# Expert products in split parts for whole tiles of one expert, with a shorter ring of weights

## Chip, cores and metric

The kernel runs on one core of one Trainium2 chip. The metric is the device time of one execution in microseconds (us).

## The reference, cut to what matters

Two trunk layers run over 256 latent tokens and 256 context tokens of 1024 features in float32. Each has a token-mixing part and a channel-mixing part. The channel mixing of the second layer, on the latent tokens alone, is a top-2-of-8 mixture of experts, and the change is in it:

```
def moe_swiglu(h, router_w, router_b, wg, wu, wd):
    logits = h.astype(jnp.float32) @ router_w.astype(jnp.float32) + router_b.astype(jnp.float32)
    top_val, top_idx = lax.top_k(logits, TOP_K)
    top_p = jax.nn.softmax(top_val, axis=-1)
    gates = jnp.sum(jax.nn.one_hot(top_idx, N_EXPERTS, dtype=jnp.float32) * top_p[..., None], axis=-2)
    gates = gates.astype(h.dtype)
    out = jnp.zeros_like(h)
    for e in range(N_EXPERTS):
        out = out + gates[..., e:e + 1] * swiglu(h, wg[e], wu[e], wd[e])
    return out
```

Here `swiglu(h, wg, wu, wd)` is `(silu(h @ wg) * (h @ wu)) @ wd`, and an expert has 3584 middle columns, so its three matrices have 3 x 1024 x 3584 float32 numbers.

## The kernel before

All work up to the router is done by other stages; the last of them, `Experts.start`, sorts the eight experts by how many tokens chose them and gathers tokens into six tiles of up to 128 rows. A tile is a list of four *quads*: `(q, s0)` is a group of 32 token slots from slot `s0` of the expert that is q-th by number of tokens. Three tiles are *whole*: all four quads are of one expert (0, 1 or 2). The other three are *mixed*: their quads are of two to three experts. `gather` picks the rows of h by products with a 0/1 matrix P, with h in two parts (`h2`), and leaves them transposed in `he`.

`go` then runs eight steps: `ORDER` goes over four quarters c of the middle columns, and for each over two *rounds* of three tiles. In round 0 two tiles are whole and one is mixed, and three experts' weights are needed; in round 1 one tile is whole, two are mixed, and five experts' weights are needed. In `step`, the gate products come first, then the up products, each in four blocks i of 256 rows of the weights. For each block SyncE (SP) issues the load of one piece per expert into a ring of `NW` buffers `wf`; a load waits until the last reader of its buffer is done. Each tile then does two rows kk of products of 448 columns for two halves. The gate sums go through SiLU on ScalarE (ACT) into `a`, VectorE (DVE) multiplies `a` by the up sums, `trans` transposes `a` on TensorE (PE) and copies it to SBUF, and the down products of 512 columns follow, in four blocks u with up to two j each. `acc` collects the four quarters. When the last quarter is done, `back` returns the rows to their tokens with products with `PT`, in two parts `oh` and `ol`, and `end` adds the result to the output.

In `products`, a whole tile is one product for each half: 128 token rows are the stationary operand and the weights are streamed. A mixed tile is four products for each half, one for each quad, with 32 token rows each:

```
for i, ps in enumerate(p):
    for j, (q, s0) in enumerate(quads):
        js = slice(32 * j, 32 * j + 32)
        self.k.mm(ps[js, 0:cols], lhs[:, js], rhs[q][i], first, last)
```

A quad's products use 32 of the array's 128 columns (a *column group*, or quarter) and write 32 of the 128 rows of `ps`. PSUM has six banks for these sums (`gu`) and two for transposes (`tr`), and all six are in use in every phase of a step.

The order in which each engine's instructions stand is not written by hand: a scheduler sets it when the program is built, from a timeline that it computes itself.

Of the kernel before, what the change touches and what calls it, by code (L numbers as in the profile page):

```python
# [10 lines left out]
F32R = mybir.dt.float32r  # L11
# [1286 lines left out]
class Experts:  # L1298

    TILES = [[(0, 0), (0, 32), (0, 64), (0, 96)], [(1, 0), (1, 32), (1, 64), (1, 96)], [(0, 128), (0, 160), (1, 128), (7, 0)],
             [(4, 0), (4, 32), (5, 0), (5, 32)], [(2, 0), (2, 32), (2, 64), (2, 96)], [(3, 0), (3, 32), (3, 64), (6, 0)]]
    ROUNDS = [(0, 1, 2), (3, 4, 5)]
    ORDER = [(r, c) for c in range(4) for r in (0, 1)]
    MORE = [[(0, 192), (0, 224)], [(1, 160), (1, 192), (1, 224)]] + [[(q, CAPS[q] + 32 * i) for i in range(n)] for q, n in
# [29 lines left out]
                    i += m // 32  # L1337
        return P

    def gather(self, pool, tiles, h2, ps, he):  # L1340

        nc, k, V = self.nc, self.k, self.nc.vector
        n = sum(32 * len(t) for t in tiles)
        P = self.select(pool, tiles)
        for kk in range(8):
            p = ps(kk)
            i = 0
            for t in range(2):
                for part in range(2):
                    k.mm(p[:, 0:n], h2[part][:, t, 128 * kk:128 * kk + 128], P[:, t], i == 0, i == 3)  # L1350
                    i += 1
            if kk % 2:
                V.tensor_copy(he[:, kk], p[:, 0:n])
            else:
                nc.scalar.activation(he[:, kk], p[:, 0:n], AF.Copy)
        out, c = [], 0
        for i, quads in enumerate(tiles):
# [12 lines left out]
            V.tensor_copy(g[0:m], p[0:m, 256:257])  # L1370
            out.append(dict(quads=quads, m=m, he=he[:, :, c:c + m], PT=pt[0:m], g=g[0:m]))
            c += m
        return out

    def start(self, pool, h2, ps):
        T = self.k.T
        self.y = T(self.mp, [128, 2, D], "ymoe")
        self.nc.gpsimd.memset(self.y, 0.0)
        self.he = T(self.mp, [128, 2, 8, 384], "he")
        self.tiles = []  # L1380
        for i in range(2):
            self.tiles += self.gather(pool, self.TILES[3 * i:3 * i + 3], h2, ps, self.he[:, i])


    def go(self, ep, pp):
# [20 lines left out]
                        self.step(tiles, c)  # L1406
            self.end()

    NW = 13

    def expert(self, q):
        if q not in self.ev:
# [11 lines left out]
    def down_weights(self, q, c, u):  # L1424

        n = min(4, 14 - 4 * u)
        w = self.T([128, 2048], "wf", bufs=self.NW)
        src = self.A["moe_w_down"][0][bass.ds(self.expert(q), 1), 896 * c:896 * c + 896, :][0].rearrange("(p j) n -> p (j n)", j=7)
        self.nc.sync.dma_start(w[:, 0:512 * n], src[:, 2048 * u:2048 * u + 512 * n])
        return [w[:, 512 * i:512 * i + 512] for i in range(n)]  # L1430

    def products(self, p, cols, tile, lhs, rhs, first, last):

        quads = tile["quads"]
        if len(quads) == 4 and len({q for q, s in quads}) == 1:
            for ps, r in zip(p, rhs[quads[0][0]]):
                self.k.mm(ps[:, 0:cols], lhs, r, first, last)
            return
        for i, ps in enumerate(p):
            for j, (q, s0) in enumerate(quads):  # L1440
                js = slice(32 * j, 32 * j + 32)
                self.k.mm(ps[js, 0:cols], lhs[:, js], rhs[q][i], first, last)

    def step(self, tiles, c):

# [1 line left out]
        experts = list(dict.fromkeys(q for t in tiles for q, s0 in t["quads"]))  # L1447
        banks = lambda: [[self.ps("gu") for s in range(2)] for t in tiles]
        a = [self.T([128, 896], "a", bufs=3) for t in tiles]
        for up in range(2):  # L1450
            ps = banks()
            for i in range(4):
                w = {q: self.up_weights("moe_w_up" if up else "moe_w_gate", q, c, i) for q in experts}
                for t, p in zip(tiles, ps):
                    for kk in range(2):
                        self.products(p, 448, t, t["he"][:, 2 * i + kk], {q: [w[q][kk][:, 448 * s:448 * s + 448] for s in range(2)] for q in w},
                                      i + kk == 0, i + kk == 4)
            for t, p, o in zip(tiles, ps, a):
                m = t["m"]
                for s in range(2):  # L1460
                    o_ = o[0:m, 448 * s:448 * s + 448]
                    if up:
                        V.tensor_tensor(o_, o_, p[s][0:m, 0:448], op=OP.mult)  # L1463
                    else:
                        nc.scalar.activation(o_, p[s][0:m, 0:448], AF.Silu)  # L1465
        aT = [self.trans(t, o) for t, o in zip(tiles, a)]
        ps = banks()
        for u in range(4):
            w = {q: self.down_weights(q, c, u) for q in experts}
            for t, p, o in zip(tiles, ps, aT):  # L1470
                for j in range(2 * u, min(2 * u + 2, 7)):
                    self.products(p, 512, t, o[:, j], {q: w[q][2 * j - 4 * u:2 * j - 4 * u + 2] for q in w}, j == 0, j == 6)
        for t, p in zip(tiles, ps):
            m, key = t["m"], id(t)
            if c == 0:
# [10 lines left out]
    def trans(self, t, a):  # L1486

        nc, k, m = self.nc, self.k, t["m"]
        o = self.T([128, 7, 128], "aT", bufs=3)
        for j0 in (0, 4):  # L1490
            n = min(4, 7 - j0)
            p = self.ps("tr")
            for j in range(n):
                k.tr(p[:, m * j:m * j + m], a[0:m, j0 + j::7], m)
            nc.scalar.activation(o[:, j0:j0 + n, 0:m], p[:, 0:m * n].rearrange("p (j m) -> p j m", m=m), AF.Copy)  # L1495
        return o[:, :, 0:m]

    def back(self, t, acc):

        nc, V, m = self.nc, self.nc.vector, t["m"]  # L1500
        for n in range(2):
            ns = slice(512 * n, 512 * n + 512)
            oh = self.T([128, 512], "oh", F32R, 2)
            ol = self.T([128, 512], "ol", F32R, 2)
# [9 lines left out]
    def end(self):  # L1514
# [16 lines left out]
        for h in range(2):  # L1531
            ns = slice(512 * h, 512 * h + 512)
            for t in range(2):
                d = self.T([128, 512], ("oh", "ol")[t], bufs=2)
# [24 lines left out]
```

## Time and profile before

| what | value |
|---|---|
| median of 3 runs | 2514.85 us (2512.44 to 2524.78) |
| the profiled execution | 2531.41 us, span 2529.6 us |
| busy over the span: TensorE, VectorE, ScalarE | 2228.6, 1105.6, 745.3 us |
| expert stage, from the first product to the last | about 1541 to 2503.5 us |
| loaded from HBM over the span | 546.71 MB |

The profiled execution is a single one; its time is 16.6 us above the median, and its rows are measured from the start of its span. A float32 product appears in the rows as two records of equal length, an fp32r product as one. Matmuls are pipelined: the duration of a record is longer than the distance from one start to the next. An operand of type fp32r is shown as f32 on TensorE's rows.

### The profile page before, as it was taken

How to read it: one execution, taken by the hardware profiler on the slowest of the kernel's cores; microseconds unless marked ns; L12 is line 12 of the kernel's file. 1: busy time of each engine (PE TensorE's matmuls, PEld its weight loads, DVE VectorE, ACT ScalarE, POOL GpSimd, SP SyncE). 2: the span in 40 equal slices, each digit the busy share in tenths (PEclk: the TensorE clock that was granted, in tenths of full speed). 3: DMA queues.
4: the chain of work that ended last, by engine and by line, in shares of the span. 5: the costliest groups of instructions: out<-in, count | busy, mean ns of one | idle time of the engine just before them, and what ended most of it. 6: DMA issues, size and time to landing. Idle time of an engine off the chain costs nothing. (4 is left out here: it accounts for less than half of the span.)

```text
span 2529.6 us, 41612 instructions
## 1 busy us (share of the span) xinstructions
PE 2228.6 (88%) x16691; PEld 1425.1 (56%) x16691; DVE 1105.6 (44%) x2168; ACT 745.3 (29%) x1549; POOL 286.6 (11%) x403
## 2 busy tenths in 40 slices
PE   5898888699979987887877759999999999999996
PEld 2787645587779976766753545434343343334332
DVE  3587868777543455878685651000010101000203
ACT  2664524444433346655541321010100000000001
POOL 3112332220000001120443020000000000000000
PEclk7998868689989988998886679999999999999998
DMA  8655475434433325425466027799969997999794
GB/s 272 197 147 159 136 264 181 123 115 126 127 107 92 93 83 156 134 85 146 126 201 211 31 84 291 285 405 414 408 261 405 415 394 273 408 412 357 312 399 190
DMA packets 320709, 570.57 MB, mean 226 GB/s; under 512 B 25423, under 2 KB 208475, under 8 KB 301563
## 3 DMA queue, kind: packets, MB, share of 16 engines
q1 hardware_dynamic: 303786, 544.46, 59.8%
q10 hardware_dynamic: 12816, 15.42, 1.8%
q0 software_dynamic: 3904, 7.94, 0.9%
q8 instruction: 133, 2.18, 0.4%
q14 instruction: 70, 0.57, 0.1%
HBM read 546.71 MB, written 21.05 MB: 224 GB/s over the span
## 5 line engine op out<-in xcount | busy, mean ns | idle before, releaser
L113 PE MATMUL gu<-wf,he 128*32 128x448 f32 (+1 forms) x3840 | 628.3, 543 | 1.1 <-DMA wf<-in_moe_w_up 1.0
L113 PEld LDWEIGHTS gu<-wf,he 128*32 128x32 f32 (+1 forms) x3840 | 242.6, 125 | 375.4 <-issue 353.6
L1463 DVE TENSOR_TENSOR a<-a,gu 128x448 f32<-128x448 f32 x48 | 29.8, 621 | 653.9 <-PE gu L113 651.4
L113 PE MATMUL gu<-wf,aT 128*32 128x512 f32 (+1 forms) x1680 | 311.2, 596 | 0.0
L103 ACT ACTIVATE wh<-wf 128x512 fp32r<-128x512 f32 (+1 forms) x279 | 184.6, 664 | 208.8 <-PE z L109 87.4
L104 DVE TENSOR_TENSOR wl<-wf,wh 128x512 fp32r<-128x512 f32 (+1 forms) x261 | 197.9, 760 | 82.0 <-ACT wh L103 77.4
L113 PEld LDWEIGHTS gu<-wf,aT 128*32 128x32 f32 (+1 forms) x1680 | 111.2, 126 | 180.5 <-issue 173.0
L108 PE MATMUL z<-hi,wh 128*128 128x256 f32 x552 | 169.3, 307 | 27.1 <-ACT wh L103 21.0
L110 PE MATMUL z<-hi,wl 128*128 128x256 f32 x552 | 167.6, 307 | 11.6 <-DVE wl L104 8.5
L109 PE MATMUL z<-lo,wh 128*128 128x256 f32 x552 | 164.6, 298 | 0.0
L1495 ACT ACTIVATE aT<-tr 128x512 f32<-128x512 f32 (+1 forms) x48 | 24.4, 542 | 377.0 <-PE tr L116 376.8
L108 PEld LDWEIGHTS z<-hi,wh 128*128 128x128 f32 x552 | 113.8, 206 | 33.6 <-ACT wh L103 24.0
L1465 ACT ACTIVATE a<-gu 128x448 f32<-128x448 f32 x48 | 26.0, 544 | 358.9 <-PE gu L113 358.9
L110 PEld LDWEIGHTS z<-hi,wl 128*128 128x128 f32 x552 | 113.4, 207 | 18.0 <-DVE wl L104 10.8
L1482 DVE TENSOR_TENSOR acc<-acc,gu 128x512 f32<-128x512 f32 x36 | 24.0, 684 | 216.4 <-PE gu L113 216.2
L1536 POOL TENSOR_TENSOR wf<-wf,ol 128x512 f32<-128x512 f32 x2 | 3.3, 1646 | 1005.0 <-DVE ol L1535 1005.0
L109 PEld LDWEIGHTS z<-lo,wh 128*128 128x128 f32 x552 | 114.0, 207 | 0.8 <-issue 0.4
L110 PE MATMUL gu<-hi,wl 128*128 128x256 f32 x320 | 97.5, 305 | 3.2 <-DVE wl L104 3.2
L108 PE MATMUL gu<-hi,wh 128*128 128x256 f32 x320 | 97.1, 303 | 1.3 <-ACT wh L103 0.9
L109 PE MATMUL gu<-lo,wh 128*128 128x256 f32 x320 | 95.0, 297 | 0.0
L993 DVE TENSOR_TENSOR itmp<-A,T 64x31 f32<-64x31 f32 (+15 forms) x248 | 89.9, 363 | 4.7
L104 DVE TENSOR_TENSOR bk<-wf,bk 128x512 fp32r<-128x512 f32 x72 | 49.8, 692 | 95.3 <-ACT bk L103 94.1
(506 smaller groups left out, 3997.8 us busy)
## 6 DMA issues: line engine op xcount, KB each, us to landing
wf<-in_moe_w_gate SPq DMA_DIRECT2D x128, 896.0 KB, 13.5
wf<-in_moe_w_up SPq DMA_DIRECT2D x128, 896.0 KB, 16.2
wf<-in_moe_w_down SPq DMA_DIRECT2D x96, 1024.0 KB, 17.3
wf<-in_w_in SPq DMA_DIRECT2D x75, 512.0 KB, 4.3
lo<-in_ada_w SPq DMA_DIRECT2D x20, 1024.0 KB, 5.5
hi<-in_ada_w SPq DMA_DIRECT2D x20, 1024.0 KB, 4.9
wf<-in_ffn_w_gate SPq DMA_DIRECT2D x32, 512.0 KB, 3.7
wf<-in_ffn_w_up SPq DMA_DIRECT2D x32, 512.0 KB, 3.7
```

The source lines that it names most:

```text
L103: self.nc.scalar.activation(hi, src, AF.Copy)
L104: (eng or self.nc.vector).tensor_tensor(lo, src, hi.bitcast(F32), op=OP.subtract)
L108: mm(ps, lhsT=lh, rhs=rh, start=first, stop=False)
L109: mm(ps, lhsT=lh, rhs=rl, start=False, stop=False)
L110: mm(ps, lhsT=ll, rhs=rh, start=False, stop=last)
L113: self.nc.tensor.matmul(ps, lhsT=l, rhs=r, start=start, stop=stop)
L993: V.tensor_tensor(tv, A32[:, i + 1:32, i:i + 1].to_broadcast([64, n, m]), T32[:, i:i + 1, 0:m].to_broadcast([64, n, m]), op=OP.mult)
L1463: V.tensor_tensor(o_, o_, p[s][0:m, 0:448], op=OP.mult)
L1465: nc.scalar.activation(o_, p[s][0:m, 0:448], AF.Silu)
L1482: V.tensor_tensor(o, o, p[n][0:m], op=OP.add)
L1495: nc.scalar.activation(o[:, j0:j0 + n, 0:m], p[:, 0:m * n].rearrange("p (j m) -> p j m", m=m), AF.Copy)
L1536: (nc.gpsimd if t else V).tensor_tensor(x[:, t, ns], x[:, t, ns], d, op=OP.add)
```

## The change

For whole tiles, each operand is cut into a high part, rounded to fp32r, and a low part, the remainder: the gathered tokens (in `gather`, `parts`), the weights (in the new method `parts`, by `split`: a copy on ACT and a subtraction on DVE), and the transposed middle columns (in `trans`). `products` then does three products, high x high, low x high and high x low, in place of one float32 product. Mixed tiles stay as they were. The tile of expert 2 comes first in round 1, the ring of pieces has 8 buffers in place of 13, and `back` and `end` use the buffers `wh` and `wl`.

```
-             [(4, 0), (4, 32), (5, 0), (5, 32)], [(2, 0), (2, 32), (2, 64), (2, 96)], [(3, 0), (3, 32), (3, 64), (6, 0)]]
+             [(2, 0), (2, 32), (2, 64), (2, 96)], [(4, 0), (4, 32), (5, 0), (5, 32)], [(3, 0), (3, 32), (3, 64), (6, 0)]]
...
+    @staticmethod
+    def whole(quads):
+        return len(quads) == 4 and len({q for q, s0 in quads}) == 1
...
         for kk in range(8):
-            p = ps(kk)
-            i = 0
+            p = ps(2 * kk)
             for t in range(2):
-                for part in range(2):
-                    k.mm(p[:, 0:n], h2[part][:, t, 128 * kk:128 * kk + 128], P[:, t], i == 0, i == 3)
-                    i += 1
+                mm(p, 0, kk, t, 0, n, t == 0, False)
+            for t in range(2):
+                mm(p, 1, kk, t, nw, n, False, t == 1)
+            if nw:
+                pl = ps(2 * kk + 1)
+                for t in range(2):
+                    mm(pl, 1, kk, t, 0, nw, t == 0, t == 1)
+                nc.scalar.activation(parts[0][:, kk], p[:, 0:nw], AF.Copy)
+                nc.vector.tensor_copy(parts[1][:, kk], pl[:, 0:nw])
             if kk % 2:
-                V.tensor_copy(he[:, kk], p[:, 0:n])
+                V.tensor_copy(he[:, kk], p[:, nw:n])
             else:
-                nc.scalar.activation(he[:, kk], p[:, 0:n], AF.Copy)
+                nc.scalar.activation(he[:, kk], p[:, nw:n], AF.Copy)
...
-    NW = 13
+    NW = 8
...
+    def parts(self, w, n):
+
+        hi, lo = [self.T([128, 1024], t, F32R, 3)[:, 0:n] for t in ("wh", "wl")]
+        self.k.split(hi, lo, w)
+        return hi, lo
 
     def products(self, p, cols, tile, lhs, rhs, first, last):
 
-        quads = tile["quads"]
-        if len(quads) == 4 and len({q for q, s in quads}) == 1:
-            for ps, r in zip(p, rhs[quads[0][0]]):
-                self.k.mm(ps[:, 0:cols], lhs, r, first, last)
+        mm, quads = self.k.mm, tile["quads"]
+        if self.whole(quads):
+            for l, r in ((0, 0), (1, 0), (0, 1)):
+                for i, ps in enumerate(p):
+                    mm(ps[:, 0:cols], lhs[l], rhs[r][:, cols * i:cols * i + cols], first and l == r, last and r == 1)
             return
...
     def trans(self, t, a):
 
         nc, k, m = self.nc, self.k, t["m"]
-        o = self.T([128, 7, 128], "aT", bufs=3)
+        whole = self.whole(t["quads"])
+        o = [self.T([128, 7, 128], n, F32R, 2) for n in ("aTh", "aTl")] if whole else [self.T([128, 7, 128], "aT", bufs=2)]
...
+            if whole:
+                k.split(o[0][:, j0:j0 + n, 0:m], o[1][:, j0:j0 + n, 0:m], src)
+            else:
+                nc.scalar.activation(o[0][:, j0:j0 + n, 0:m], src, AF.Copy)
```

The change also moves instructions. The first place is on PE, in round 0, in the last block of the up products, where both programs have two whole tiles (experts 0 and 1) and one mixed tile (two quads of expert 0, one of 1, one of 7). In the rows `128x448` is a product of a whole tile and `32x448` one of a quad; `gu` is the sum, the name behind the arrow the weights: `wf` a piece as loaded, `wh` and `wl` its parts. Before, with 15602 and 15603 as the mixed tile's two halves:

```order
L113 MATMUL gu_15600<-wf_15696,he_15218 128x448
L113 MATMUL gu_15601<-wf_15696,he_15218 128x448
L113 MATMUL gu_15600<-wf_15696,he_15218 128x448
L113 MATMUL gu_15601<-wf_15696,he_15218 128x448
L113 MATMUL gu_15602<-wf_15694,he_15218 32x448 x2
L113 MATMUL gu_15602<-wf_15696,he_15218 32x448
L113 MATMUL gu_15602<-wf_15698,he_15218 32x448
L113 MATMUL gu_15603<-wf_15694,he_15218 32x448 x2
L113 MATMUL gu_15603<-wf_15696,he_15218 32x448
L113 MATMUL gu_15603<-wf_15698,he_15218 32x448
```

The four quads of a half stand together, and sixteen products of quads follow each other in all. In the change, with 15815 and 15816 as the mixed tile's halves:

```order
L113 MATMUL gu_15815<-wf_16003,he_2859_15218 32x448 x2
L113 MATMUL gu_15813<-wh_16029,he_2860_15219 128x448
L113 MATMUL gu_15814<-wh_16029,he_2860_15219 128x448
L113 MATMUL gu_15813<-wh_16029,he_2861_15220 128x448
L113 MATMUL gu_15814<-wh_16029,he_2861_15220 128x448
L113 MATMUL gu_15815<-wf_16005,he_2859_15218 32x448
L113 MATMUL gu_15815<-wf_16007,he_2859_15218 32x448
L113 MATMUL gu_15816<-wf_16003,he_2859_15218 32x448 x2
L113 MATMUL gu_15813<-wl_16030,he_2860_15219 128x448
L113 MATMUL gu_15814<-wl_16030,he_2860_15219 128x448
L113 MATMUL gu_15816<-wf_16005,he_2859_15218 32x448
L113 MATMUL gu_15816<-wf_16007,he_2859_15218 32x448
```

The quads of one half are now cut in two, and products of a whole tile stand between the pieces. The second place is on PE in round 1, in the second block of the gate products. Before, expert 2's whole tile (15894, 15895) stands between the two mixed tiles (15892, 15893 and 15896, 15897):

```order
L113 MATMUL gu_15892<-wf_15989,he_15218 32x448 x2
L113 MATMUL gu_15892<-wf_15991,he_15218 32x448 x2
L113 MATMUL gu_15893<-wf_15989,he_15218 32x448 x2
L113 MATMUL gu_15893<-wf_15991,he_15218 32x448 x2
L113 MATMUL gu_15894<-wf_15993,he_15218 128x448
L113 MATMUL gu_15895<-wf_15993,he_15218 128x448
L113 MATMUL gu_15894<-wf_15993,he_15218 128x448
L113 MATMUL gu_15895<-wf_15993,he_15218 128x448
L113 MATMUL gu_15896<-wf_15995,he_15218 32x448 x3
L113 MATMUL gu_15896<-wf_15997,he_15218 32x448
L113 MATMUL gu_15897<-wf_15995,he_15218 32x448 x3
L113 MATMUL gu_15897<-wf_15997,he_15218 32x448
```

In the change, with 16351 and 16352 as the whole tile:

```order
L113 MATMUL gu_16351<-wh_16484,he_2889_15366 128x448
L113 MATMUL gu_16352<-wh_16484,he_2889_15366 128x448
L113 MATMUL gu_16351<-wh_16484,he_2890_15367 128x448
L113 MATMUL gu_16352<-wh_16484,he_2890_15367 128x448
L113 MATMUL gu_16353<-wf_16466,he_2888_15365 32x448 x2
L113 MATMUL gu_16354<-wf_16466,he_2888_15365 32x448 x2
L113 MATMUL gu_16351<-wl_16485,he_2889_15366 128x448
L113 MATMUL gu_16352<-wl_16485,he_2889_15366 128x448
L113 MATMUL gu_16353<-wf_16468,he_2888_15365 32x448 x2
L113 MATMUL gu_16354<-wf_16468,he_2888_15365 32x448 x2
```

The first two quads of the mixed tile now stand ahead of the whole tile's last two products, the other two behind them. The third place is on DVE in round 0, where up ends and down begins. Before, the six products with `a` of this step follow each other, and nothing else stands among them:

```order
L1463 TENSOR_TENSOR a_15436<-a_15436,gu_15598 128x448
L1463 TENSOR_TENSOR a_15436<-a_15436,gu_15599 128x448
L1463 TENSOR_TENSOR a_15437<-a_15437,gu_15600 128x448
L1463 TENSOR_TENSOR a_15437<-a_15437,gu_15601 128x448
L1463 TENSOR_TENSOR a_15438<-a_15438,gu_15602 128x448
L1463 TENSOR_TENSOR a_15438<-a_15438,gu_15603 128x448
```

In the change, from the last tile's products with `a` on:

```order
L1488 TENSOR_TENSOR a_15523<-a_15523,gu_15815 128x448
L104 TENSOR_TENSOR wl_16146<-wf_16121,wh_16145 128x1024
L1488 TENSOR_TENSOR a_15523<-a_15523,gu_15816 128x448
L104 TENSOR_TENSOR aTl_16072<-tr_16073,aTh_16071 128x512
L104 TENSOR_TENSOR aTl_16072<-tr_16080,aTh_16071 128x384
L104 TENSOR_TENSOR aTl_16087<-tr_16088,aTh_16086 128x512
L104 TENSOR_TENSOR wl_16156<-wf_16121,wh_16155 128x1024
L104 TENSOR_TENSOR wl_16188<-wf_16181,wh_16187 128x1024
L104 TENSOR_TENSOR aTl_16087<-tr_16095,aTh_16086 128x384
L104 TENSOR_TENSOR wl_16198<-wf_16181,wh_16197 128x1024
L104 TENSOR_TENSOR wl_16208<-wf_16183,wh_16207 128x1024
```

The subtractions for the weights' low parts and for the low parts of the transposed `a` now stand in one queue with the products with `a`.

## Rows read from the trace of the kernel before

**Rows 1.** The page: TensorE's busy time, granted clock and DMA share by slices.

```profile
PE   5898888699979987887877759999999999999996
PEclk7998868689989988998886679999999999999998
DMA  8655475434433325425466027799969997999794
```

**Rows 2.** Stretches: length, busy time by engine, granted clock, DMA share, GB/s.

```profile
1650.00:1776.00 126.00, 125.00 (x874) 48.71 (x874) 3.73 (x6) 12.89 (x24) 0.00 (x0) 1.00 1.02 410
1541.00:2503.50 962.50, 957.38 (x5709) 379.22 (x5708) 67.50 (x105) 65.01 (x118) 0.00 (x0) 1.00 0.92 366
```

**Rows 3.** Groups by form, from 1500 us on: busy us, mean ns, idle before.

```profile
L113 PE MATMUL gu<-wf,he 128*32 128x448 f32 x3072 | 329.5, 542 | 1.0 <-DMA wf<-in_moe_w_up 1.0
L113 PE MATMUL gu<-wf,he 128*128 128x448 f32 x768 | 308.0, 549 | 0.2 <-DMA wf<-in_moe_w_gate 0.2
L113 PE MATMUL gu<-wf,aT 128*32 128x512 f32 x1344 | 162.3, 595 | 0.0
L113 PE MATMUL gu<-wf,aT 128*128 128x512 f32 x336 | 152.3, 600 | 0.0
...
L116 PE MATMUL tr<-k_ident,a 128*128 128x128 f32 x168 | 26.7, 294 | 4.0 <-DVE a L1463 2.5 <-ACT aT L1495 1.5
```

**Rows 4.** PE by form, 1558.7 to 1563.9 us: whole tiles alone.

```profile
L113 PE MATMUL gu<-wf,he 128*128 128x448 f32 x15 | 5.8, 539 | 0.0
```

**Rows 5.** PE by form, 1544.3 to 1547.4 us: the first mixed block.

```profile
L113 PE MATMUL gu<-wf,he 128*32 128x448 f32 x32 | 3.2, 542 | 0.0
```

**Rows 6.** Timeline around 1550 us, start and length; PEld are weight loads.

```profile
1549.15 3.48 PE L113 MATMUL gu<-wf,he 128*128 128x448 f32 x8
...
1550.75 0.14 PEld L113 LDWEIGHTS gu<-wf,he 128*32 128x32 f32 x2 [0.65 <-issue]
```

**Rows 7.** Timeline of PE, fp32r products of 512 columns in the dense layer.

```profile
901.27 0.39 PE L109 MATMUL dn<-bk,ah 128*128 128x512 f32 x1
901.51 0.40 PE L110 MATMUL dn<-bk,al 128*128 128x512 f32 x1
...
902.90 0.40 PE L110 MATMUL dn<-bk,AT 128*128 128x512 f32 x1
```

**Rows 8.** Timeline of PE, fp32r products of 256 columns.

```profile
1190.48 0.28 PE L108 MATMUL z<-hi,wh 128*128 128x256 f32 x1
...
1191.08 0.28 PE L110 MATMUL z<-hi,wl 128*128 128x256 f32 x1
```

**Rows 9.** Timeline around 2380 us: back's fp32r products between sets of quads.

```profile
2379.22 0.95 PE L113 MATMUL gu<-wf,he 128*32 128x448 f32 x6
...
2380.11 0.50 PE L113 MATMUL tr<-oh,PT 128*128 128x512 f32 x1
...
2380.44 0.40 PE L113 MATMUL tr<-ol,PT 128*128 128x512 f32 x1
...
2380.77 1.33 PE L113 MATMUL gu<-wf,he 128*32 128x448 f32 x12
```

**Rows 10.** Groups by form: DVE and ACT on float32 tiles of 512 and 1024 columns.

```profile
L104 DVE TENSOR_TENSOR bk<-wf,bk 128x512 fp32r<-128x512 f32 x65 | 45.0, 692 | 87.7 <-ACT bk L103 86.6
...
L1231 DVE SCALAR_TENSOR_TENSOR hf<-xl,hrs,scr 128x1024 f32<-128x1024 f32 x2 | 2.5, 1281 | 0.0
...
L1233 ACT ACTIVATE h<-hf 128x1024 fp32r<-128x1024 f32 x2 | 2.1, 1048 | 5.0 <-POOL hf L1232 5.0
```

**Rows 11.** DMA issues: count, KB each, median us to landing.

```profile
wf<-in_moe_w_gate SPq DMA_DIRECT2D x128, 896.0 KB, 13.5
...
wf<-in_moe_w_down SPq DMA_DIRECT2D x96, 1024.0 KB, 17.3
...
lo<-in_ada_w SPq DMA_DIRECT2D x20, 1024.0 KB, 5.5
```

**Rows 12.** Groups by form, from 1500 to 1541 us: the gather.

```profile
L113 PE MATMUL he<-P,h 128*128 128x384 f32 x64 | 15.1, 406 | 6.5 <-DVE P L1335 6.5
...
L1353 DVE COPY he<-he 128x384 f32<-128x384 f32 x8 | 4.5, 557 | 9.3 <-PE he L113 8.7
```

More of the change, by code (lines that the diff above doesn't have):

```diff
@@ L1370, in gather @@
             V.tensor_copy(g[0:m], p[0:m, 256:257])
-            out.append(dict(quads=quads, m=m, he=he[:, :, c:c + m], PT=pt[0:m], g=g[0:m]))
+            rows = [x[:, :, c:c + m] for x in parts] if self.whole(quads) else [he[:, :, c - nw:c - nw + m]]
+            out.append(dict(quads=quads, m=m, he=rows, PT=pt[0:m], g=g[0:m]))
             c += m
@@ L1378, in start @@
         self.nc.gpsimd.memset(self.y, 0.0)
-        self.he = T(self.mp, [128, 2, 8, 384], "he")
         self.tiles = []
         for i in range(2):
-            self.tiles += self.gather(pool, self.TILES[3 * i:3 * i + 3], h2, ps, self.he[:, i])
+            tiles = self.TILES[3 * i:3 * i + 3]
+            n = sum(map(self.whole, tiles))
+            he = T(self.mp, [128, 8, 384 - 128 * n], f"he{i}")
+            parts = [T(self.mp, [128, 8, 128 * n], f"he{i}{j}", F32R) for j in range(2)]
+            self.tiles += self.gather(pool, tiles, h2, ps, he, parts)
     def go(self, ep, pp):
@@ L1441, in products @@
                 js = slice(32 * j, 32 * j + 32)
-                self.k.mm(ps[js, 0:cols], lhs[:, js], rhs[q][i], first, last)
+                mm(ps[js, 0:cols], lhs[0][:, js], rhs[q][:, cols * i:cols * i + cols], first, last)
     def step(self, tiles, c):
@@ L1449, in step @@
         a = [self.T([128, 896], "a", bufs=3) for t in tiles]
+        turn = lambda t, w, j, n: self.parts(w[t["quads"][0][0]][j], n) if self.whole(t["quads"]) else {q: w[q][j] for q in w}
         for up in range(2):
@@ L1455, in step @@
                     for kk in range(2):
-                        self.products(p, 448, t, t["he"][:, 2 * i + kk], {q: [w[q][kk][:, 448 * s:448 * s + 448] for s in range(2)] for q in w},
-                                      i + kk == 0, i + kk == 4)
+                        self.products(p, 448, t, [x[:, 2 * i + kk] for x in t["he"]], turn(t, w, kk, 896), i + kk == 0, i + kk == 4)
             for t, p, o in zip(tiles, ps, a):
@@ L1471, in step @@
                 for j in range(2 * u, min(2 * u + 2, 7)):
-                    self.products(p, 512, t, o[:, j], {q: w[q][2 * j - 4 * u:2 * j - 4 * u + 2] for q in w}, j == 0, j == 6)
+                    self.products(p, 512, t, [x[:, j] for x in o], turn(t, w, j - 2 * u, 1024), j == 0, j == 6)
         for t, p in zip(tiles, ps):
@@ L1494, in trans @@
                 k.tr(p[:, m * j:m * j + m], a[0:m, j0 + j::7], m)
-            nc.scalar.activation(o[:, j0:j0 + n, 0:m], p[:, 0:m * n].rearrange("p (j m) -> p j m", m=m), AF.Copy)
-        return o[:, :, 0:m]
+            src = p[:, 0:m * n].rearrange("p (j m) -> p j m", m=m)
+            if whole:
+                k.split(o[0][:, j0:j0 + n, 0:m], o[1][:, j0:j0 + n, 0:m], src)
+            else:
+                nc.scalar.activation(o[0][:, j0:j0 + n, 0:m], src, AF.Copy)
+        return [x[:, :, 0:m] for x in o]
     def back(self, t, acc):
@@ L1502, in back @@
             ns = slice(512 * n, 512 * n + 512)
-            oh = self.T([128, 512], "oh", F32R, 2)
-            ol = self.T([128, 512], "ol", F32R, 2)
+            oh, ol = [self.T([128, 1024], x, F32R, 3)[:, 0:512] for x in ("wh", "wl")]
             nc.scalar.activation(oh[0:m], acc[:, ns], AF.Copy, scale=t["g"])
@@ L1533, in end @@
             for t in range(2):
-                d = self.T([128, 512], ("oh", "ol")[t], bufs=2)
+                d = self.T([128, 1024], ("wh", "wl")[t], bufs=3)[:, 0:512]
                 V.scalar_tensor_tensor(d, y[:, t, ns], r[:, t:t + 1], gate[:, h], op0=OP.mult, op1=OP.mult)
```

7 lines of the change are left out of this document (5 added, 2 removed).

## Prediction

> **What bounds the kernel now.** I read the page first: its slices show where TensorE is busy and at which clock [rows 1]. From slice 25 on, the expert stage, TensorE is busy in nine tenths of the time or more and the granted clock is full, while the DMA engines are nearly as busy. The stretches [rows 2] settle which of the two it is: over the whole stage PE is busy for 957.4 of 962.5 us at granted clock 1.00, and the DMA queues for 0.92 of it; in the first step of round 1 alone they are saturated at 410 GB/s. So the stage is bound by TensorE, with the weights' stream close behind in round 1. DVE works 67.5 us and ACT 65.0 us of 962.5: both are free. Last I read the groups by form [rows 3], which give the counts. A float32 product appears as two records: 768 records are the 384 gate and up products of whole tiles, 336 the 168 down products; the 128x32 records are products of mixed tiles, each with one quarter (a column group) of the array.
>
> **What TensorE's work costs now.** Fifteen records of whole tiles in a row take 5.8 us [rows 4]; without the last one's 0.54 that is 0.376 per record, 0.752 per 448-column product, and by columns 0.859 per 512-column one. The 32 column-group records in [rows 5] take 3.2 us: four run side by side, eight deep, 0.38 apart. So a *set*, up to four quarters at once, costs as much as a whole product. A set counts in full even when it is not full: in [rows 6] eight records, of which two (one quarter, both passes) stand alone among six of whole tiles, take 3.48 us. Less the 0.54 of the last, the starts span 2.94; six whole records alone would span 5 x 0.376 = 1.88. The lone quarter adds 1.06 us: 0.752 for itself, and 0.31 for changing to column groups and back.
>
> I count in the orders of both programs: whole products; between two whole products the depth of sets (how many products the fullest quarter has); and changes to sets and back. Before: 384 + 168 whole products, 407 sets of 448 columns and 178 of 512, 117 changes. That is 288.8 + 144.3 + 306.1 + 152.9 + 37 = 929 us, and with the transposes' 26.7 [rows 3] 956, against 957.4 busy. The count holds.
>
> **The change, part by part.**
>
> *Three products instead of one.* The 552 whole products become 1152 of 448 columns and 504 of 512, on fp32r operands. Rows of that kind: 512 columns start (902.90 - 901.27) / 7 = 0.233 us apart [rows 7], 256 columns (1191.08 - 1190.48) / 5 = 0.12 [rows 8]; 448 lie between, at 0.205. Sum 236.2 + 117.4 = 353.6 against 433.1: TensorE saves 79.5 us. Were 448 columns as slow as 512, it would save 47.
>
> *The order of TensorE's queue.* This is the dearest part, and the diff does not show it. In the new order the sets of the mixed tiles no longer follow each other: pieces of them stand between the hi and lo products of whole tiles (the two places in the section on the change). Round 0 now has 39 to 41 changes a step instead of 12 or 13, round 1 has 25 instead of 15, and quarters that ran as one set are spread over two. In total 533 sets of 448 columns instead of 407, 209 of 512 instead of 178, 262 changes instead of 117. The extra sets cost 126 x 0.752 + 31 x 0.859 = 121.4 us. For a change between sets and fp32r products there is a row, too: from 2379.22 to 2380.77 [rows 9] lie one set and two 512-column fp32r products, 1.55 - 0.752 - 0.466 = 0.33 us more. I take 0.32: 145 x 0.32 = 46.4 us. Bounds: if a third of the new lone quarters still found company, minus 56; nothing in the rows makes a lone one dearer than 1.06.
>
> The Trainium skill's TensorEngine Tiling (Array Packing), Key Properties, says that a change of tiling mode drains the engine, without a figure. By it a change costs what the last record outlasts its spacing, 0.54 - 0.376 = 0.16 each way on [rows 4], which also holds for the 448-column fp32r products that the trace lacks; the sum stays. The same skill's TensorE: Matmul & The Clock Gate, The mechanism, has matmuls start strictly in program order. By that, quarters behind a busy one wait, I would count 620 sets before and 784 after, and the term would be 164 x 0.78 = 128 instead of 121. The trace speaks against it: the 32 records of [rows 5] stand in an order that would need five sets one after another, and they took the time of four.
>
> *Splits on ACT and DVE.* Each of 12 whole-tile steps adds 16 splits of 896 columns and 7 of 1024: one ACT copy and one DVE subtraction each. DVE takes 0.69 for 512 and 1.28 for 1024 columns [rows 10], so about 1.13 for 896; ACT 1.05 for 1024. DVE gets 12 x (18.1 + 9.0) = 325 us of some 1070, ACT less. In a block of four pieces of round 0, DVE needs 4.5 us and TensorE 10, so steady blocks hide it. The cover is gone at the joint of up and down (third place): behind the last up set, DVE has one wl and two products with a (1.28 + 1.4) ahead of the first lo part of the transposed a, then four such parts and five wl (2.8 + 6.4), while TensorE has about 2 us of transposes and 24 fp32r products, 5.6 us. That is a wait of 3 us in a step of round 0, I say 2 in round 1: 4 x 5 = 20 us. Below nothing; above, twice that.
>
> *Ring of 8 instead of 13.* A gate or up piece is 896 KB, a down piece up to 1024 KB [rows 11]. A round 1 step loads 5 x 10752 KB = 55.05 MB, 134 us at 410 GB/s; its work on TensorE by the counts is 29.5 + 91 + 8 + 3 = 132 us. In round 0 it is 33 MB, 81 us, against 130. Round 0 leaves 8 - 3 = 5 pieces, 11 us, ahead. So TensorE stays the bound, by little; I add 2 us per round 1 step for pieces that are late, 8 us. Below nothing. Above: a piece that is asked for only when it is needed costs its own landing, about 5 us [rows 11], instead of 2.2; see the third rival.
>
> *Gather.* The matmuls that pick the rows have as many columns as before (per block 2 x 768 against 4 x 384), 15.1 us in 64 [rows 12]. Copies grow from 16 to 48, shorter ones on two engines, 0.56 for 384 columns [rows 12], beside the matmuls. 128-column fp32r products have no row; 32 of them at two passes add 2 us. I take 1, bounds 0 and 4: this delays the first weights, so it is on the path.
>
> **Sum.** -79.5 + 121.4 + 46.4 + 20 + 8 + 1 = +117 us. The profiled execution took 2531.4 us (span 2529.6), so 2649 for one like it; it lies 16.6 above the median of the runs shown, 2514.85, on which the forecast stands: 2632 us, slower by 4.7%.
>
> **The rivals.**
>
> *Slower (the forecast), chance 0.82.* Its own range is the one given below.
>
> *Faster: TensorE takes the quarters together whatever stands between them.* Then the sets fall to their full packing, 384 + 168 (23 and 10 fewer than now, -26 us), the changes cost nothing new, and -79.5 - 26 + 29 remains, limited by the weights: 352 MB at 410 GB/s are 860 us against 962. That gives about 2438. For it: quarters do run beside each other in [rows 5]. Against it: [rows 6], where a lone one among whole products had all four quarters' time to itself. It decides from the point where an extra lone set with its changes costs under a third of the 1.06 us. Chance 0.06.
>
> *Slower by far: the short ring starves round 1.* Five of eight slots are in use there, SP issues in ring order, and if in each of 12 blocks a step one piece waits for its landing, 4 x 12 x 2.8 = 134 us come on top of the sum without its 8: 2758. For it: in [rows 2] the queues are already saturated in round 1, with a deeper ring. Against it: the three free slots hold 6.7 us of transfers, and a whole expert's piece is free as soon as it is split. Chance 0.08.
>
> *No change: the terms cancel*, if half of the lone sets are not paid and no wait is added: 2502 to 2527. Chance 0.04.
>
> **Range and chances.** Low: the forecast without waits and with a third of the sets less, 2514.85 + 88 - 56 + 20 = 2567. High: all upper bounds but the starved ring, 88 + 40 + 60 + 4 = 192, 2707. Two executions of this kernel differ by some 0.5%, 12.6 us, which is about what can be told from no change. Faster 0.06 (the column groups' case alone), same 0.04, slower 0.82 + 0.08 = 0.90.
>
> **What would show it.** The gate and up records of whole tiles: 1152 single ones, 0.2 us apart in a row. Column-group records in stretches of two or three sides, with 0.1 us lost on entering and leaving each. PE busy about 1045 us in the stage, pairs of rounds some 28 us longer, the DMA share down to about 0.82, DVE busy near 400 us. I am wrong if the stage's PE busy time is below 960 us (the order does not cost), if PE waits for wf in round 1 by more than 10 us a step (the ring), if it waits for wl in steady blocks (the splits), or if the granted clock leaves 1.00 in the stage.

## The result and the profile after

The changed kernel takes 2646.1 us (2642.9 to 2650.4, 4 runs), the kernel before beside it 2518.7 us (2512.4 to 2524.8, 4 runs): ratio 1.0486, 95% interval 1.0448 to 1.0524. The forecast of 2632 us, slower by 4.7%, held. The profiled execution took 2648.85 us at a span of 2647.0, where the sum had 2649 for one like the profiled one of before.

The page of the changed kernel, in the lines of [rows 1]:

```profile
PE   4898787889799878878787699999999999999997
PEclk7998778899899889988857699999999999999998
DMA  8654574444323254254651267997699869986795
```

By the page TensorE stays busy and at its full clock from slice 25 on. What changed is below it: the DMA line stands at 9 in 7 of these 16 slices, where it did in 10. The stretches (length, busy time by engine, granted clock, DMA share, GB/s), first four steps, round 0 and round 1 in turn, then the whole stage:

```profile
1538.20:1665.40 127.20, 125.46 (x670) 63.20 (x666) 60.49 (x64) 54.74 (x65) 0.00 (x0) 1.00 0.61 227
1665.40:1804.30 138.90, 133.98 (x899) 57.57 (x895) 27.66 (x30) 30.31 (x42) 0.00 (x0) 1.00 1.01 403
1804.30:1935.60 131.30, 130.77 (x665) 66.24 (x665) 61.35 (x62) 50.73 (x59) 0.00 (x0) 0.99 0.65 246
1935.60:2072.70 137.10, 133.59 (x899) 57.46 (x895) 31.62 (x36) 28.15 (x36) 0.00 (x0) 1.00 1.01 403
...
1538.20:2617.40 1079.20, 1056.67 (x6269) 490.10 (x6265) 381.65 (x408) 322.49 (x393) 0.00 (x0) 1.00 0.83 322
```

The first two steps and the same stage of the kernel before, from first to last product:

```profile
1537.80:1654.20 116.40, 115.86 (x575) 47.74 (x577) 4.61 (x10) 10.54 (x18) 0.00 (x0) 1.00 0.86 339
1654.20:1775.00 120.80, 119.80 (x853) 46.80 (x845) 3.73 (x6) 9.12 (x18) 0.00 (x0) 1.00 1.02 410
...
1537.80:2503.80 966.00, 960.88 (x5719) 380.72 (x5717) 68.68 (x110) 65.01 (x118) 0.00 (x0) 1.00 0.92 366
```

So the stage grew by 113.2 us: 95.8 are busy time of PE and 17.4 are idle time. The span grew by 117.4; 3.8 of the rest lie behind the last product (25.8 us before, 29.6 now), 0.4 ahead of the first. A step of round 0 and one of round 1 together take 266 to 269 us, against 237 to 239. DVE and ACT, at 382 and 322 us of 1079, are far from being full.

Groups by form, from 1500 us on (busy us, mean ns of one, idle before), against [rows 3]; records overlap, so busy times of groups don't add up:

```profile
L113 PE MATMUL gu<-wf,he 128*32 128x448 f32 x3072 | 443.8, 545 | 0.0
...
L113 PE MATMUL gu<-wh,he 128*128 128x448 f32 x768 | 200.0, 382 | 9.6 <-ACT wh L103 9.1
L113 PE MATMUL gu<-wf,aT 128*32 128x512 f32 x1344 | 191.7, 597 | 0.0
...
L113 PE MATMUL gu<-wl,he 128*128 128x448 f32 x384 | 121.7, 397 | 4.7 <-DVE wl L104 4.0
```

The mixed tiles' products are the same 3072 and 1344 records, each as long as before. Yet there are 114.3 and 29.4 us more in which at least one of them runs: fewer of them run side by side. The timeline of PE (start, length) shows how:

```profile
1698.91 0.97 PE L113 MATMUL gu<-wh,he 128*128 128x448 f32 x4
1699.81 1.70 PE L113 MATMUL gu<-wf,he 128*32 128x448 f32 x8
1701.44 0.67 PE L113 MATMUL gu<-wl,he 128*128 128x448 f32 x2
1702.03 3.24 PE L113 MATMUL gu<-wf,he 128*32 128x448 f32 x32
```

The eight records are two quarters, four passes each, where [rows 5] had four quarters side by side. Then two low products of a whole tile, then quarters again. From 1699.81 to 1702.03 it is 2.22 us; four passes at 0.376 and two products at 0.203 (the distance of such records in a row, where the forecast had 0.205) are 1.91, and the change from column groups to the whole array and back is the other 0.31.

PE's own waits in the stage (us in total, times, longest):

```profile
PE gu L113 <- ACT wh L103: 9.1, 9, 2.0
PE tr L113 <- DVE ymoe L1541: 4.5, 3, 2.0
PE gu L113 <- DVE wl L104: 4.0, 3, 1.4
PE tr L116 <- DVE a L1488: 2.4, 3, 0.8
...
PE gu L113 <- ACT aTh L103: 1.3, 4, 0.4
```

None is large. The longest of the first kind stand where the work turns from one sum to the next. In the first step of round 1, where gate turns to up (start, length, what):

```profile
1708.47 0.54 ACT L1490 ACTIVATE a<-gu 128x448 f32<-128x448 f32 x1 [0.21 <-PE gu L113]
1708.91 1.78 ACT L103 ACTIVATE wh<-wf 128x896 fp32r<-128x896 f32 x2
...
1709.90 1.08 PE L113 MATMUL gu<-wh,he 128*128 128x448 f32 x4 [1.47 <-ACT wh L103]
```

The copy of the first up piece stands in ACT's queue behind the last SiLU, which waits for PE's last gate sum, and so PE is idle for 1.47 us. The same wait is in all four steps of round 1. Where a step of round 0 begins it is 1.3 to 2.0 us; there copies and additions into `acc` (in the first step, work of `gather`) stand ahead of the splits on ACT and DVE. No late piece is in these waits: one of expert 2 that lands just when it is wanted, at 1696.16 us, leaves PE idle for 0.1 us.

The wait of 2.0 us, which ends at 1804.3 us, is soon followed by this stretch (in the columns of [rows 2]):

```profile
1805.80:1809.20 3.40, 3.40 (x11) 3.02 (x10) 3.01 (x4) 1.93 (x3) 0.00 (x0) 0.50 1.03 404
```

The granted clock is 0.50, that is 1.2 GHz, and products of whole tiles start 0.373 us apart and not 0.203. A second such stretch begins at 2249.5 us, behind a wait of 1.47 us. Together they are 6.8 us of the stage and cost about half of that.

### The profile page after: what moved, and what is told of

It reads as the page before. It is cut to its first block, busy times and chain, and to the rows that moved or that the text cites. A ratio compares the mean times of both kernels' runs of the same rounds, so it can differ in the third digit from the quotient of the medians.

```text
span 2647.0 us, 43795 instructions
## 1 busy us (share of the span) xinstructions
PE 2329.3 (88%) x17275; PEld 1537.7 (58%) x17275; DVE 1425.6 (54%) x2484; ACT 1007.4 (38%) x1841; POOL 288.7 (11%) x403
## 4 chain that ended last, share of the span: by engine, by line
PE 45%; DVE 8%; DMA 5%; ACT 2%; issue 2%; POOL 1%; SPq 0%; ACTq 0%; DVEq 0%; POOLq 0%
PE gu L113 35%; DMA wf<-in_moe_w_gate 2%; DVE wl L104 1%; DMA lo<-in_ada_w 1%; DMA wf<-in_moe_w_up 1%; ACT wh L103 1%; PE tr L116 1%; DVE itmp L993 1%; PE he L1352 1%; DVE T L995 1%; PE z L110 1%; PE z L108 1%; DVE A L985 1%; PE z L109 1%; PE A L113 1%
## 5 line engine op out<-in xcount | busy, mean ns | idle before, releaser
L104 DVE TENSOR_TENSOR wl<-wf,wh 128x512 fp32r<-128x512 f32 (+2 forms) x537 | 505.8, 952 | 701.5 <-ACT wh L103 553.3
L103 ACT ACTIVATE wh<-wf 128x512 fp32r<-128x512 f32 (+2 forms) x555 | 449.8, 822 | 824.7 <-PE gu L113 297.6
L113 PE MATMUL gu<-wf,he 128*32 128x448 f32 x3072 | 443.8, 545 | 0.0
L113 PEld LDWEIGHTS gu<-wf,he 128*32 128x32 f32 x3072 | 123.8, 109 | 219.3 <-issue 207.3
L113 PE MATMUL gu<-wh,he 128*128 128x448 f32 x768 | 200.0, 382 | 9.6 <-ACT wh L103 9.1
L113 PEld LDWEIGHTS gu<-wh,he 128*128 128x128 f32 x768 | 137.8, 190 | 94.4 <-issue 47.9
L113 PE MATMUL gu<-wf,aT 128*32 128x512 f32 x1344 | 191.7, 597 | 0.0
L113 PE MATMUL gu<-wl,he 128*128 128x448 f32 x384 | 121.7, 397 | 4.7 <-DVE wl L104 4.0
L109 PEld LDWEIGHTS z<-lo,wh 128*128 128x128 f32 x552 | 114.3, 207 | 0.8 <-issue 0.4
L113 PEld LDWEIGHTS gu<-wf,aT 128*32 128x32 f32 x1344 | 49.0, 109 | 107.9 <-issue 107.2
L113 PEld LDWEIGHTS gu<-wl,he 128*128 128x128 f32 x384 | 63.9, 188 | 78.8 <-issue 51.2
```

The lines of the kernel that those rows point to most:

```text
L103: self.nc.scalar.activation(hi, src, AF.Copy)
L104: (eng or self.nc.vector).tensor_tensor(lo, src, hi.bitcast(F32), op=OP.subtract)
L109: mm(ps, lhsT=lh, rhs=rl, start=False, stop=False)
L113: self.nc.tensor.matmul(ps, lhsT=l, rhs=r, start=start, stop=stop)
```

## The experiments

**Theory:** the order of TensorE's queue is the cost, sets that are not full and changes of mode (from products of the whole array to column groups and back). **Rivals:** the ring of 8 pieces starves round 1; the splits hold the products up. Each run was timed beside the kernel before, so ratios compare runs; the kernel before took 2526 to 2528 us there.

**1. The order alone.** The products of a step are held in the order of the code, each behind the last:

```diff
+        i = self.nc.tensor.matmul(ps, lhsT=l, rhs=r, start=first, stop=last)
+        if self.pin:
+            if self.prev is not None:
+                self.k.tc.add_manual_dep(i.ins, self.prev.name, ..., reason="order")
+            self.prev = i.ins
```

(The line with `...` is shortened; `products` calls this method, and `self.pin` is set for the eight steps. This order is called *held* below.)

> The change with each product of a step held behind the product before it in the code, so that the four column groups of a mixed tile's products follow one another; nothing else is touched. By the orders there are 392 sets of mixed records of 448 columns (533 in the changed kernel), 169 of 512 (209) and 105 changes of mode (262). Theory, that the order of the products is the cost: 141 x 0.752 + 40 x 0.859 + 157 x 0.32 = 191 us less of PE, busy 1057 to about 866 in the stage. Then the transfers bound it: the kernel before moved the same weights in 966 us at a share of 0.92, at full share about 890. So the stage takes 890 to 970 and the time is 2460 to 2535 us. Rival, that the ring of 8 pieces or the waits for the split hold the stage: it stays at 2600 us or more, with PE idle in the place of the busy time. Rival, that records of one column group each overlap whatever the order: 2646, and PE as busy as before.

Measured: 2512.9 us, ratio 0.9941 (0.9917 to 0.9965). The loss of 4.9% is gone, and the change is 0.6% faster than before. The theory holds. Steps of both rounds, then the stage:

```profile
1767.90:1870.70 102.80, 101.58 (x665) 64.12 (x665) 61.15 (x62) 51.44 (x60) 0.00 (x0) 1.00 0.86 332
1870.70:2003.10 132.40, 123.06 (x900) 55.47 (x896) 33.06 (x39) 26.38 (x35) 0.00 (x0) 1.00 1.02 410
...
1531.10:2480.40 949.30, 909.75 (x6271) 484.78 (x6269) 383.82 (x412) 322.67 (x394) 0.00 (x0) 0.99 0.94 367
```

Round 0 fell from 131 to 103 us a step, as the counts say. Round 1 fell only from 137 to 132: by the same prices its *records' sum* (all products, sets and changes in their order) would allow 110, and the queues stand at 410 GB/s. PE's busy time went down by 147 us and not by 191. A quarter whose piece is late leaves the others running alone, which reads as busy; where the transfers are spread evenly (experiment 5) it is 864 us, close to the 866 expected here. The bound of round 1 has passed to the transfers.

**2. The ring alone**, in the kernel before, whose order stays the same:

```diff
-    NW = 13
+    NW = 8
```

> The kernel before with a ring of 8 pieces in place of 13, and nothing else: the products stand in the same order. Theory, that the short ring is a small part of the loss: 2519 to 2540 us, PE as busy as before (957 to 961) with up to 20 us more of idle time. Rival, that the ring is most of the loss: 2580 us or more, with PE waiting for wf in round 1's steps, where five experts share the ring.

Measured: 2562.3 us, ratio 1.0144 (1.0113 to 1.0174): between the two, a little nearer the rival. A step of round 0 stays at 116 to 118 us, one of round 1 goes from 121 to 131 or 132:

```profile
1654.40:1785.40 131.00, 128.55 (x854) 48.91 (x846) 3.72 (x6) 9.12 (x18) 0.00 (x0) 1.00 1.02 410
```

And the group of the mixed records, from 1500 us on, against the first of [rows 3]:

```profile
L113 PE MATMUL gu<-wf,he 128*32 128x448 f32 x3072 | 360.3, 542 | 5.8 <-DMA wf<-in_moe_w_up 3.9 <-DMA wf<-in_moe_w_gate 2.0
```

Of 36 us, 31 stand in the busy time of this group (360.3 against 329.5) and 5 in idle time. The expected sign of a short ring, PE waiting for wf, was the wrong one to look for: a wait of one column group is hidden under the busy time of the others. The timeline of PE shows one:

```profile
1696.14 1.67 PE L113 MATMUL gu<-wf,he 128*32 128x448 f32 x9
1698.33 0.98 PE L113 MATMUL gu<-wf,he 128*32 128x448 f32 x8 [0.51 <-DMA wf<-in_moe_w_up]
```

In 1.67 us there is room for four passes of four quarters, 16 records, and nine stand there; of the whole wait, only the last 0.51 us are idle time. The Trainium skill's TensorEngine Tiling (Array Packing), Key Properties, says that tiles of the array operate independently, and the trace agrees: while the late quarters waited, the others went on, 0.376 us apart, for four passes.

**3. Changes alone.** In the held order, the halves of a piece become the outer loop and the tiles the inner one:

```diff
-                for t, p in zip(tiles, ps):
-                    for kk in range(2):
+                for kk in range(2):
+                    for t, p in zip(tiles, ps):
```

(and the same for `j` in the down products).

> The same held order, but the two halves of a piece (kk, and j in the down products) are the outer loop and the tiles the inner one, so that PE goes from the whole tiles to the mixed ones and back twice in a piece and not once: 189 changes of mode (105 in the held order), with 385 and 168 sets (392 and 169), nearly the same. Theory, that a change there and back costs 0.32 us of PE: 84 x 0.32 - 7 x 0.75 = about +22 us of busy time on PE beside the held order; the time rises by 0 to 22 us, as far as the transfers leave PE no slack. Rival, that a change costs nothing: busy time the same within 5 us.

Measured: 2555.4 us, ratio 1.0122 (1.0086 to 1.0158), so 1.8% above the held order, and the stage 990.0 us with PE busy for 924.6, 14.8 more. That sum mixes in round 1, where pieces are now held longer. A step of round 0, which no transfer binds, is clean:

```profile
1783.10:1891.30 108.20, 106.40 (x670) 62.02 (x666) 61.38 (x62) 51.77 (x61) 0.00 (x0) 1.00 0.83 315
```

With 11 changes more it is 5.4 us longer and 4.8 us busier, which would be 0.44 to 0.49 us for a change there and back. The starts of the records say less:

```profile
1788.24 1.08 PE L1460 MATMUL gu<-wh,he 128*128 128x448 f32 x4
...
1790.86 1.71 PE L1460 MATMUL gu<-wf,he 128*32 128x448 f32 x16
1792.51 0.68 PE L1460 MATMUL gu<-wh,he 128*128 128x448 f32 x2
```

Twelve products and four passes take 4.27 us here, 0.33 more than 12 x 0.203 + 4 x 0.376. Taken so over all changes of the two steps, one costs 0.34 us, so that 11 are 3.7 of the 5.4 us. The rest lies in other gaps between starts, 0.7 us of it ahead of the transposes and 0.5 ahead of high and low products. Changes cost about what the sum had.

**4. Nine pieces**, in the held order, paid for with two buffers for the parts:

```diff
-    NW = 8
+    NW = 9
-        hi, lo = [self.T([128, 1024], t, F32R, 3)[:, 0:n] for t in ("wh", "wl")]
+        hi, lo = [self.T([128, 1024], t, F32R, 2)[:, 0:n] for t in ("wh", "wl")]
```

(and two buffers in `back` and `end`, too).

> The held order with a ring of 9 pieces in place of 8, paid for with two buffers each for the high and low weights in place of three. Theory, that the held order is bound by transfers which wait for a free piece: 10 to 30 us less than the held order. Rival, that the ring has enough: the same within 5 us. Rival, that the third buffer of the parts matters: 10 to 40 us more, with PE's waits for the split longer.

Measured: 2502.4 us, ratio 0.9906 (0.9876 to 0.9936), about 9 us less, at the low edge of what the theory said. The intervals of the two overlap; the steps agree, round 1's at 130.2 to 130.9 us instead of 132.3, about the time of one piece at 410 GB/s:

```profile
1872.90:2003.10 130.20, 121.86 (x900) 53.69 (x896) 34.07 (x40) 26.40 (x35) 0.00 (x0) 1.00 1.02 410
```

The third buffer is not missed, as far as the two changes together can tell.

**5. Even rounds.** The quads are dealt out so that each round reads four experts (three and five before), in the held order:

```diff
+    TILES = [[(0, 0), (0, 32), (0, 64), (0, 96)], [(0, 128), (0, 160), (4, 0), (4, 32)], [(3, 0), (3, 32), (3, 64), (6, 0)],
+             [(1, 0), (1, 32), (1, 64), (1, 96)], [(2, 0), (2, 32), (2, 64), (2, 96)], [(1, 128), (5, 0), (5, 32), (7, 0)]]
```

(the two lines that they replace are left out).

> The held order, with the quads dealt out so that each round has whole tiles and mixed ones of four experts (before three experts in round 0 and five in round 1): round 0 has experts 0, 3, 4 and 6, round 1 has 1, 2, 5 and 7, still three whole and three mixed tiles. Sets and changes stay (388, 168 and 104; 392, 169 and 105 in the held order). In the held order round 1's steps take 132 us each at 410 GB/s and a DMA share of 1.02, round 0's 103 us at 332 GB/s and 0.87. Theory, that transfers bound round 1 alone and the ring is too short to load for it in round 0: both rounds' steps take 105 to 113 us, the stage 870 to 900, the time 2435 to 2470 us. Rival, that it is the order or the split of round 1's tiles: each step keeps its sum, 2500 to 2520 us. Rival, that the mixed tiles' waits for late pieces spread over both rounds: 2480 to 2500.

> The even rounds with a ring of 9 pieces and two buffers each for the parts. Theory, that with even rounds the transfers are no longer held by the ring: within 5 us of the even rounds with 8 pieces. Rival, that a piece still gives what it gave in the uneven rounds (10 us): 8 to 15 us less.

Measured: 2459.2 us, ratio 0.9715 (0.9689 to 0.974), and with nine pieces 2439.9 us, 0.9642 (0.9618 to 0.9666). The stage of each:

```profile
1550.20:2433.60 883.40, 863.64 (x6273) 465.58 (x6266) 376.68 (x408) 317.43 (x393) 0.00 (x0) 1.00 0.99 395
```

```profile
1534.70:2410.00 875.30, 857.81 (x6271) 459.83 (x6266) 380.80 (x408) 322.29 (x392) 0.00 (x0) 1.00 1.00 399
```

Steps take 103 to 114 us, but for one of 122 in each with back's work in it; PE and the transfers are both nearly full. The first theory holds. With nine pieces this version is 3.6% faster than the kernel before, and the fastest tried. By the medians the ninth piece gives 19 us, more than the 5 that I expected. Of 25.9 us between the two profiled spans, though, 8.1 are in the stage and 15.5 ahead of it, where I changed nothing. TensorE's granted clock differs there: with 8 pieces it stood at 1.2 GHz for 485 us ahead of the stage, with nine for 457. Half of these 27 us would be most of the 15.5; why the clock differed is not shown. In the stage the ninth piece gives 8 us.

**6. Even rounds, free order.** The same `TILES` in the changed kernel, nothing held:

> The changed kernel with the even rounds and its products in the scheduler's own order (530 and 240 scattered sets of mixed records, 228 changes; 533, 209 and 262 in the changed kernel). By the sums of the records in their order PE takes 1062 us (1050 in the changed kernel). Theory, that the order of the products sets the changed kernel's time and the ring costs it only what its steps stand over that sum (some 25 us, nearly all in round 1): 2625 to 2650 us, with DMA busy at 0.80 to 0.85 in both rounds. Rival, that uneven rounds with a short ring are the cost: 2540 to 2590 us.

Measured: 2655.6 us, ratio 1.0507 (1.0468 to 1.0547), the same as the changed kernel. The stage:

```profile
1534.70:2626.00 1091.30, 1064.41 (x6272) 496.00 (x6265) 382.17 (x408) 320.28 (x393) 0.00 (x0) 1.00 0.85 320
```

Against the even rounds in the held order this is the cleanest test of the order: the same weights, tiles and ring, 142 sets of 448 and 72 of 512 columns and 124 changes more. By the sum's prices that is 208 us; PE's busy time differs by 201 and the medians by 196. The rival is out. The time is 6 us above the theory's range, for my own side guess fell too: the queues are down to 0.85, and the stage still stands 29 us above its records' sum (1062), as the changed kernel's does (1050).

**7. The two parts alone.** The kernel before in the held order and with 8 pieces, against experiment 1:

> The kernel before with the products held in the order of the code and a ring of 8 pieces: the held order without the split (394 sets, 173 sets, 116 changes, where the held order of the changed kernel has 392, 169 and 105). Theory, that the two parts themselves save PE's time (79.5 us by the forecast's count) where the order is equal: PE's busy time in round 0's steps is 10 to 14 us longer than the held order's 102 us, round 1's steps are bound by transfers at 410 GB/s (130 us) in both, and the time is 2545 to 2575 us, 30 to 60 above the held order. Rival, that the split only moves the cost: 2500 to 2525 us.

Measured: 2555.6 us, ratio 1.0111 (1.0064 to 1.0159), 43 us above experiment 1. One step of each round:

```profile
1780.30:1895.60 115.30, 114.92 (x577) 47.64 (x577) 7.01 (x11) 7.01 (x13) 0.00 (x0) 1.00 0.79 300
1895.60:2026.60 131.00, 123.65 (x854) 46.40 (x846) 8.00 (x13) 6.20 (x12) 0.00 (x0) 1.00 1.02 410
```

In round 0 the split saves 12.5 us a step (115.3 against 102.8), and 13.3 us of PE's busy time. In round 1 it saves nothing, since both wait for the same 410 GB/s.

**8. The splits doubled.** Each product is held at the place that it has in the changed kernel, and each piece is split twice:

```diff
-        self.k.split(hi, lo, w)
+        for i in range(2):
+            self.k.split(hi, lo, w)
```

> The changed kernel with its products held in the very order that they have in it (528 and 208 scattered sets, 256 changes of mode, by the records' sum 1043 us against 1050), and every weight piece split twice into the same two parts: ACT's copy and DVE's subtraction (949 and 1090 ns) run twice before a product may read them. The changed kernel's stage is 1079 us long, 30 above that sum. Theory, that the waits for the split are some 20 of these 30: twice the work makes them 20 to 40 us longer, 2660 to 2690 us. Rival, that the 30 are the short ring in round 1: 2640 to 2652 us.

Measured: 2696.4 us, ratio 1.0672 (1.0638 to 1.0706), 1.8% above the changed kernel and 6 us above the theory's range. PE's wait for the copies alone:

```profile
PE gu L1462 <- ACT wh L103: 43.6, 35, 3.4
```

It was 9.1; PE's idle time in the stage goes from 22.5 to 54.2 us. At the turn from gate to up PE waits 1.5 to 2.8 us in seven of eight steps, and there are waits inside round 1's blocks, too. The splits do stand in the open, and not at the joint of up and down only. But waits are not all of it. The stage:

```profile
1537.60:2665.80 1128.20, 1074.00 (x6265) 489.80 (x6266) 668.26 (x676) 572.10 (x667) 0.00 (x0) 0.98 0.80 308
```

It is 49.0 us longer, 31.7 of them idle time and 17.3 busy time, though its records' sum is 7 us less. The granted clock is 0.98: TensorE stood at 1.2 GHz for 47.8 us, in the changed kernel for 6.8. Half of the difference, 20 us, is what that can cost.

**9. Six pieces**, in the changed kernel's own order, held in the same way:

> The changed kernel's own order of products, held (533 and 208 sets, 262 changes), with a ring of 6 pieces in place of 8. In the kernel before, 5 pieces less made a step of round 1 10 us longer, about the time of 5 x 0.92 MB at 410 GB/s (11.2 us), and a step of round 0 not at all. Theory, that round 1 of the changed kernel is bound by transfers already (137 us at 403 GB/s): 2 pieces less cost 2 x 0.92 MB / 0.41 = 4.5 us a step, four steps, 18 us: 2660 to 2670 us. Rival, that its order of products bounds round 1 and the ring has slack: 2644 to 2652 us.

Measured: 2665.8 us, ratio 1.0542 (1.0509 to 1.0575), 0.5% above the changed kernel, with intervals that overlap. The steps tell more: round 1's are 2.5 to 5.5 us longer, 16.8 in all, round 0's 4.4 in all. The second of round 1, against 137.1 us at 403 GB/s:

```profile
1945.50:2088.10 142.60, 136.47 (x896) 58.73 (x896) 33.69 (x38) 27.31 (x36) 0.00 (x0) 0.99 1.00 393
```

TensorE stood at 1.2 GHz for 17.1 us of this stage, against 6.8; by steps that can be worth 3.4 of the 16.8. The rest is some 3.4 us a step: the ring does bind round 1, at a little under the 4.5 us of two missing pieces.

## Why the prediction was right, step by step

**TensorE's order** (+121.4 and +46.4): right, and nearly the whole of it. Holding the order gave back 133 us by the medians; experiment 6 against 5 measured 201 us where the same prices say 208.

**Changes of mode**: the row at hand gave 0.33, the changed kernel's timeline 0.31, experiment 3 0.34 by starts of records. The prediction quoted the Trainium skill's TensorEngine Tiling (Array Packing), Key Properties, by which a change of mode drains the engine; worked out as an estimate, 0.16 each way. With that, 0.32, the trace agrees.

**Three products** (-79.5): right. Two of three whole tiles stand in round 0, so a step there should save 2/3 x 79.5 / 4 = 13.3 us; 12.5 were measured (experiment 7). 448 columns cost 0.203 us, by rows that the trace before lacked.

With these three PE's busy time was to grow by 88; it grew by 95.8, to 1057 instead of 1045. About 3.4 of that are the two stretches at 1.2 GHz, which the sum did not have. That the whole sum, 117, met the growth of the profiled span, 117.4, is luck: busy time is 8 us more than forecast, the waits are 11 less, and the tail adds 4.

**Waits for the split** (+20) **and the ring** (+8): 28 together, against 17.4 us of new idle time; by the sum of the records in their order the stage stands 30 above it. The size is right, the place is not. The joint of up and down, where I put all of the 20, has 4.3 us of PE's idle time, under 1 us a step. Some 13 us lie ahead of high and low products of gate and up: 1.3 to 2.0 us where a step of round 0 begins, and 1.5 where gate turns to up in round 1. The mechanism is the one that I gave, splits in one queue behind the work on the last sums, but at other joints. Steady blocks do hide the splits, as I had said, but for one wait of 0.7 us.

For the ring, what it costs depends on the order. In the kernel before it cost 36 us, 9 a step of round 1 on the mean and not 2. In the changed kernel it could cost at most the 6 us by which each of round 1's steps stands above its sum, since the scattered order is nearly as slow as the transfers. Of the 30 us above the sum, idle time is 22.5 and the clock 3.4; what is left for late pieces hidden as busy time is no more than the counts can tell. How much of the 8 was right stays open: two pieces less add 21 us to the stage, and even rounds did not lower what it stands above its sum.

**Gather** (+1): 0.4 at the start of the stage. **The tail** was not in the sum: 3.8 us behind the last product. In the trace two things stand there: back's products wait 1.8 us at once for DVE's `ymoe` (0.6 in the kernel before), and from 2622.5 to 2628 us they run at a granted clock of 0.50, which can cost half of 5.5 us. Neither was tried apart.

**The range.** Its low end, 2567, is said to be without waits, yet holds the 20 us for the splits; without them it is 2547. In the high end 40 are the splits at twice their 20; the 60 for the ring have no working.

**The rivals.** The starved ring (2758) was out by size, not by kind: 9 us a step of round 1 in experiment 2, where the rival had 33. The cancelled terms (2502 to 2527) did not come. Column groups that pack by themselves (2438) did not come either: experiments 5 and 6 put a price of 196 us on the order. The bound named there, weights at 410 GB/s and 860 us, is near: held order, even rounds and nine pieces, which pack them by hand, need 875 us for the stage, at 399 GB/s. That their 2439.9 us meet 2438 is chance.

**The signs that I named:** pairs of rounds 28 to 30 us longer (28), DMA share 0.83 (0.82), DVE 382 us (400), all as said. The clock's mean in the stage was 1.00, but it fell twice for 3.4 us, each time soon after one of PE's longer waits. PE's wait for wf over 10 us a step was no usable sign, by experiment 2.

## What to carry to other kernels

Before a change that alternates forms of products on TensorE, count in the queue's real order how full each set of column groups is and how often the form changes: the same products cost 200 us more or less by it. An order that a scheduler makes can be held with dependences, and then the bound moves on: here to transfers in one of two rounds, which dealing the work out evenly by weights, not by tiles, took away. A kernel with 13 pieces of lead hides an uneven load that one with 8 shows.

## What the runs showed that I had not expected

A late weight for one column group hardly shows as PE's idle time: in experiment 2 it is 31 us of busy time and 5 of idle. Busy time of PE is no proof that PE is the bound when column groups are in use; length of a step against its records' sum is. The weights' stream reached 410 GB/s at a DMA share of 1.02 in the saturated steps with 8, 9 and 13 pieces; in the scattered order it was 400 to 403 with 8 pieces and 390 to 394 with 6. And a wait of PE may cost more than its length: with the splits doubled 32 us more were idle, and 41 us more ran at 1.2 GHz besides.
